# A hybrid decoder layer on one core: VectorE work cut and moved in the attention half, output weights prepared over three filler steps a block, and the gather placed ahead of the experts' choice

## The chip, the core and the metric

The kernel runs on one core of a Trainium2 chip. The metric is device time in microseconds for one execution of the whole layer. TensorE (PE) multiplies matrices into PSUM, VectorE (DVE), ScalarE (ACT) and GpSimd (POOL) work on tiles in SBUF and PSUM, and SyncE (SP) issues most of the transfers. Each engine runs its own list of instructions in order and waits for others by semaphores.

## The reference, cut to what matters

1024 tokens of width 1024 (S = D = 1024) go through one layer:

```
h    = rms_norm(x, norm1_w) * (1 + sc1) + sh1            # sh1, sc1, g1, sh2, sc2, g2 = silu(c) @ w_ada + b_ada
q, kv, gates, B, C, u = split(h @ w_in)                  # 512 + 6*128 + 24 + 3*512 columns
o    = sum over 3 branches of sigmoid(gate) * attention  # compressed blocks, 16 selected blocks, window of 512
                                                         # 8 query heads, 2 kv heads, bias by distance
y    = B * causal_conv3(C * u)
x    = x + g1 * (rms_norm per 64 columns of [o, y]) @ w_out
h2   = rms_norm(x, norm2_w) * (1 + sc2) + sh2
g    = argmax of 8 group probabilities; e1, e2 = best 2 of the group's 8 experts
x    = x + g2 * sum of g_prob * e_prob * (silu(h2 @ w1[e]) * (h2 @ w3[e])) @ w2[e]
```

There are 64 experts; their weights, w1 and w3 of 1024 x 512 and w2 of 512 x 1024 in float32, are 402.65 MB. All inputs and outputs are float32.

## The kernel before

**Order of the work.** The Python code issues instructions; a scheduler then orders them on each engine by what they wait for, so the code's order is only a start. `tc.issue_after(...)` pins an instruction behind another.

**Front (to about 228 us).** The adaLN vectors, the norm of x, and the first projections run. Projections are three float16 products each (high and low halves of both factors, L367 to L369). `cmp_post` makes the compressed keys: square on ScalarE, mean on VectorE, power -1/2 on GpSimd, scaling into `jk` on VectorE (L608), then a transpose on TensorE (L611). L193 is TensorE's work for the table of near biases and shares the PSUM tag `mx`. `rstd_of` (L635) gives 1/sqrt(mean square) for a 128 x 512 block with one Newton step, three VectorE instructions from L644 to L646.

**The attention loop (228 to 707 us).** A unit is one head on one half of the queries: units 0 to 7 are half 0, 8 to 15 half 1. Each unit has 9 (half 0) or 17 (half 1) slots, 208 in all. A slot is `scores` (TensorE into PSUM `st`), `weights` (two exponentials on ScalarE, P in float32 and PH in float16, then PL = P - PH, of six slots two on VectorE and four on GpSimd, L874) and, two slots later, `values` (PH and PL times the values into PSUM `acc`). At the end of each of a unit's three branches `take` divides by the sum and multiplies by the gate (L881 to L883, then L889 or L892). Between the slots run four other things:

- `prepare(u + 1)`: the row maxima of the next unit. QB gets a copy of the queries (L794); TensorE writes scores into `mx`; VectorE reduces them (L820, L835, L843) into `parts`; the compressed scores give the third maximum (L849) with a floor (L850); `Mh` (L852) goes back to TensorE (L857).
- `merge(pr)` after every second unit normalises two heads: square on ScalarE (L959), sum on VectorE, power on GpSimd (L964), multiply on VectorE (L965), and six slots later a transpose on TensorE (L971).
- In half 0 the filler `conv_steps`: projections and the short convolution, 2.75 steps a slot. Its post-processing is VectorE work (L746 to L763), the first tap at L748.
- In half 1 the filler `second_half`, 0.8 steps a slot. First `out_prepare`: eight blocks of 128 rows of w_out are scaled (L1075), rounded (L1077) and their rests taken (L1079, half on VectorE, half on GpSimd), one block a step. Then `out_part` (384 products L1121 to L1123 in all), `logits` and `route(0)` for the first 512 tokens, and `out_part` for the others. What the loop has not used up runs behind it.

**Transition (740 to 785 us).** `logits` of the last four token tiles, then `route(1)`: group choice G (L1186), the group's expert logits (L1191, L1194), top two (L1197, L1198), ranks by a triangular product (L1215, L1218), places, and one table product (L1271) with eight columns per row: token number, two expert places, two weights, a norm factor. Its result `tab0` gives the token numbers `toki0` (L1446); `rows_in(0)` gathers 2 x 128 rows by them (GpSimd, L1467); `group(0)` makes one-hot matrices Sm (L1484, L1485), the weights Sw (L1495 to L1497) and the scaled rows xh and xl (L1490, L1491); `take_in(0)` selects the rows of two experts by products (L1515) and applies the adaLN factors (L1520, L1523).

**Expert stage (to the end).** 32 pairs P of experts: `up(P)` (64 products, L1533), `silu_mul` (L1456), `down(P - 1)` (L1546), `turn(P)` (transposes of hid, L1556), `take_in(P + 1)`, `turn_weights`, `give`. The weights come in 2 MB transfers on SP in a fixed order through a handful of buffers (`stream`, `put`, L1024); a transfer into a buffer waits until the products that read it are done.

Of the kernel before, what the change touches and what calls it, by code (L numbers as in the profile page):

```python
# [69 lines left out]
def tile_layer(tc, A, out, dbg=None):  # L70
# [386 lines left out]
    V.tensor_scalar(nwc[:, 0:1], nwc[:, 0:1], HD ** -0.5 / WS, None, op0=ALU.mult)  # L457
    V.tensor_scalar(nwc[:, 1:3], nwc[:, 1:3], 1.0 / WS, None, op0=ALU.mult)
# [36 lines left out]
    tab0 = qa.tile([128, 2, 8], F32, name="tab0")  # L495
# [3 lines left out]
    V.memset(crow[:, :, 1:3], -1.0)  # L499

# [37 lines left out]
    def cmp_post(kvi):  # L538
        pw, w1n, w2n = (("cmp_pos_k", "cmp_k_w1", "cmp_k_w2"), ("cmp_pos_v", "cmp_v_w1", "cmp_v_w2"))[kvi]

        def post(p, b):
# [57 lines left out]
            if kvi == 0:  # L599
# [5 lines left out]
                ACT.activation(jk, pk[:, 0:64], AF.Square, accum_out=sk[:, 0:1])  # L605
                V.tensor_scalar(sk[:, 0:1], sk[:, 0:1], 1.0 / HD, EPS, op0=ALU.mult, op1=ALU.add)
                POOL.tensor_tensor(sk[:, 1:2], sk[:, 0:1], mhalf[:, 0:1], op=ALU.pow)
                V.scalar_tensor_tensor(jk, pk[:, 0:64], sk[:, 1:2], knc, op0=ALU.mult, op1=ALU.mult)  # L608
# [26 lines left out]
    def rstd_of(sq, tag="mx"):  # L635
# [9 lines left out]
        V.tensor_scalar(t, t, -0.5, 1.5, op0=ALU.mult, op1=ALU.add)  # L645
        V.tensor_mul(r, r, t)  # L646
# [49 lines left out]
    def gate_job(idx):  # L696
# [17 lines left out]
        V.reciprocal(gf, gf)  # L714
# [18 lines left out]
    def conv_steps():  # L733

        for i in range(4):
# [8 lines left out]
            def u_post(p, b, i=i, z=z, y=y):  # L744
# [3 lines left out]
                V.tensor_scalar(ys, zs, convw[:, i, 2:3], None, op0=ALU.mult)  # L748
# [5 lines left out]
            def b_post(p, b, i=i, y=y):  # L754
                ys = y[:, b * 512:(b + 1) * 512]
                V.tensor_mul(ys, p, ys)
                sq = square(ys, 1.0)
                yield
                yield
                r = rstd_of(sq)  # L760
                V.tensor_mul(ys, ys, r)
                ACT.activation(MH[b][:, 4 + i, :], ys, AF.Copy)
                V.tensor_sub(ML[b][:, 4 + i, :], ys, MH[b][:, 4 + i, :])  # L763
# [15 lines left out]
    for q in Tcs:  # L779
        V.memset(q, 0.0)  # L780
    ident2 = aw.tile([128, 128], F16, name="ident2", bufs=1)
    V.memset(ident2, 0.0)
    V.tensor_tensor(ident2[:, 0:63], identh[:, 0:63], identh[:, 64:127], op=ALU.add)
# [3 lines left out]
    def prepare(u):  # L787
# [6 lines left out]
        V.tensor_copy(QB[0:64, :], tq[hp:hp + 64, :])  # L794
# [54 lines left out]
        V.tensor_reduce(M[:, :, 2], pc[:, 0:256].rearrange("p (i n) -> p i n", i=4)[:, :, 0:63], axis=AX.X, op=ALU.max)  # L849
        V.tensor_scalar(M[:, :, 2], M[:, :, 2], MFLOOR, None, op0=ALU.max)  # L850
# [26 lines left out]
    def take(u, acc, n, gi):  # L877
# [3 lines left out]
        V.tensor_scalar(r, av[:, :, 64], 1e-27, None, op0=ALU.max)  # L881
        V.reciprocal(r, r)
        V.tensor_mul(r, r, gates[:, half * 4:half * 4 + 4, h * 3 + gi])  # L883
# [68 lines left out]
    def merge(pr):  # L952
# [12 lines left out]
        V.tensor_tensor(sq8, o8, so[:, :, None].to_broadcast([128, 8, 64]), op=ALU.mult)  # L965
# [88 lines left out]
    def out_prepare():  # L1054
# [16 lines left out]
        for i, k in enumerate(ORDER):  # L1071
# [8 lines left out]
            yield  # L1080
# [78 lines left out]
    def route(hb):  # L1159

        rt = R["rt"]
# [13 lines left out]
        def row(ap):  # L1175
            return ap[:, None, :].to_broadcast([128, 4, ap.shape[-1]])
        mx, ix = tile_(8, "mx"), tile_(8, "ix", U32)
# [4 lines left out]
        gid, gp, z, w0, w1c, pos, okg, t0, far = (W[:, :, i:i + 1] for i in (0, 3, 4, 5, 6, 9, 12, 15, 16))  # L1182
# [3 lines left out]
        V.tensor_tensor(G, row(io64[:, 0:8]), wide(gid, 8), op=ALU.is_equal)  # L1186
        ex = tile_(8, "ex")
# [6 lines left out]
        V.tensor_reduce(ein, el.rearrange("p t g e -> p t e g"), axis=AX.X, op=ALU.add)  # L1194
# [13 lines left out]
        V.tensor_copy(GA[:, ts, 0:8], G)  # L1208
        pr = ps(tag)

        if hb:
            PE.matmul(pr[:, 0:288], onesb, R["GS"][:, None, :].to_broadcast([128, 4, 72]), start=True, stop=True)
        for i in range(4):
            t = 4 * hb + i
            PE.matmul(pr[:, i * 72:(i + 1) * 72], trib, GA[:, t, :], start=(t == 0), stop=True,  # L1215
                      skip_group_check=True)
            if i < 3:
                PE.matmul(pr[:, (i + 1) * 72:288], onesb, GA[:, t:t + 1, :].to_broadcast([128, 3 - i, 72]),  # L1218
                          start=False, stop=True, skip_group_check=True)
# [498 lines left out]
```

## Time and profile before

| what | value |
|---|---|
| median of 3 runs | 1729.34 us (1725.88 to 1734.08) |
| the profiled execution | 1726.6 us |
| its span (first to last instruction) | 1724.8 us |
| granted TensorE clock in it, mean | 0.964 |
| busy: TensorE / VectorE / ScalarE / GpSimd | 1540.9 / 746.5 / 498.1 / 351.2 us |
| moved by DMA | 480.83 MB |

Rows of the timeline read: start, duration, engine, line, operation, output<-inputs, shape, and in brackets how long the engine had stood idle and what released it. Rows of groups read: count, then busy time and mean nanoseconds of one, then idle time ahead of them with its releasers. Rows of waits read: who waited for whom, total, times, longest.

### The profile page before, as it was taken

What the parts mean: (1) busy time and instruction counts of PE and PEld (TensorE: products, weight loads), DVE (VectorE), ACT (ScalarE), POOL (GpSimd) and SP (SyncE); (2) the same over time, 40 slices, a digit from 0 to 9 for tenths busy, and PEclk for the clock granted to TensorE, in tenths of its full rate; (3) what the DMA queues carried; (4) which work ended last, traced back from release to release, by engine and by line L of the source; (5) the groups of instructions that cost most, each with busy time, mean ns of one, the idle gap of its engine ahead of it and who ended that gap; (6) DMA issues with size and microseconds to landing.
All of it is one profiled execution on the core that took longest, in us unless ns stands there. A gap on an engine that the chain in (4) does not pass through costs nothing. (4 is left out here: it accounts for less than half of the span.)

```text
span 1724.8 us, 24591 instructions
## 1 busy us (share of the span) xinstructions
PE 1540.9 (89%) x9839; PEld 733.7 (43%) x9839; DVE 746.5 (43%) x1767; ACT 498.1 (29%) x968; POOL 351.2 (20%) x347
## 2 busy tenths in 40 slices
PE   5979899889879998959999999999999999899995
PEld 3434454445446665533434343343343333343431
DVE  3747876676796766554312223123203113121211
ACT  4654655445546564321112001011101002011000
POOL 4232543343454445220000000000000000000000
PEclk8989999999999999979999999999999999999998
DMA  9338531100241120759999999999999999999992
GB/s 348 100 113 258 179 92 34 51 23 15 69 151 41 35 79 22 299 196 395 421 426 425 428 426 426 428 425 427 427 426 426 428 425 427 425 427 427 426 428 122
DMA packets 84628, 480.83 MB, mean 279 GB/s; under 512 B 12551, under 2 KB 46552, under 8 KB 58652
## 3 DMA queue, kind: packets, MB, share of 16 engines
q1 hardware_dynamic: 76620, 461.16, 66.3%
q0 software_dynamic: 7744, 18.03, 2.9%
q8 instruction: 79, 1.29, 0.3%
q14 instruction: 41, 0.34, 0.1%
q10 hardware_dynamic: 144, 0.00, 0.0%
HBM read 473.20 MB, written 14.35 MB: 283 GB/s over the span
## 5 line engine op out<-in xcount | busy, mean ns | idle before, releaser
L1533 PE MATMUL ps<-wr,xs 128*64 128x512 f32 x2048 | 451.5, 596 | 0.0
L1546 PE MATMUL ps<-wr,hT 128*64 128x512 f32 x1024 | 260.3, 614 | 42.4 <-DMA wr<-in_w_dram 40.9
L1533 PEld LDWEIGHTS ps<-wr,xs 128*64 128x64 f32 x2048 | 158.3, 137 | 287.4 <-issue 251.7
L1520 ACT ACTIVATE xs<-ps,sh2p,a2p 128x128 f32<-128x128 f32 x128 | 55.0, 454 | 569.2 <-DVE xs L1523 569.1
L1456 DVE TENSOR_TENSOR hid<-ps,hid 128x512 f32<-128x512 f32 x32 | 22.1, 691 | 412.8 <-PE ps L1533 412.8
L1583 POOL DMA_INDIRECT out_dram<-xg,toki x16 | 15.9, 997 | 791.5 <-DVE xg L1582 790.8
L1546 PEld LDWEIGHTS ps<-wr,hT 128*64 128x64 f32 x1024 | 80.1, 141 | 215.4 <-issue 150.6
L874 POOL TENSOR_TENSOR PL<-P,PH 128x384 f16<-128x384 f32 (+3 forms) x138 | 128.5, 937 | 188.7 <-ACT PH L870 84.8
L1549 DVE TENSOR_TENSOR y<-ps,lt 128x512 f32<-128x512 f32 x64 | 44.3, 692 | 252.0 <-PE ps L1546 252.0
L868 ACT ACTIVATE P<-st 128x512 f32<-128x512 f32 (+3 forms) x208 | 98.4, 473 | 135.8 <-PE st L926 99.1
L1578 PE MATMUL sum<-y,CT 128*128 128x512 f32 x256 | 115.3, 593 | 0.0
L367 PE MATMUL pp<-hi,wh 128*128 128x512 f16 x272 | 106.0, 391 | 4.0 <-ACT hi L435 4.0
L368 PE MATMUL pp<-lo,wh 128*128 128x512 f16 x272 | 106.1, 390 | 0.0
L369 PE MATMUL pp<-hi,wl 128*128 128x512 f16 x272 | 105.8, 389 | 0.0
L870 ACT ACTIVATE PH<-st 128x512 f16<-128x512 f32 (+3 forms) x208 | 98.2, 472 | 3.1 <-DVE PL L874 2.0
L1455 ACT ACTIVATE hid<-ps 128x512 f32<-128x512 f32 x32 | 19.1, 597 | 200.9 <-PE ps L1533 200.9
L1515 PE MATMUL ps<-Sm,xh 128*128 128x128 f16 x512 | 62.4, 222 | 9.0 <-ACT xh L1490 9.0
L1578 PEld LDWEIGHTS sum<-y,CT 128*128 128x128 f32 x256 | 46.1, 190 | 46.8 <-issue 46.0
L1523 DVE TENSOR_SCALAR xs<-ps,a2p,sh2p 128x128 f32<-128x128 f32 x128 | 49.6, 407 | 35.5 <-ACT xs L1520 28.2
L1515 PE MATMUL ps<-Sm,xl 128*128 128x128 f16 x512 | 62.3, 222 | 1.8 <-DVE xl L1491 1.8
L945 PE MATMUL acc<-VH,PH 128*128 128x65 f16 x528 | 59.3, 196 | 4.2 <-DVE ot L892 4.0
L916 PE MATMUL st<-QA,KA 128*128 128x512 f16 (+1 forms) x192 | 61.5, 321 | 1.2 <-ACT PH L870 0.9
(438 smaller groups left out, 2546.5 us busy)
## 6 DMA issues: line engine op xcount, KB each, us to landing
wr<-in_w_dram SPq DMA_DIRECT2D x189, 2048.0 KB
ada<-in_w_ada_dram SPq DMA_DIRECT2D x32, 512.0 KB
raw<-in_w_in_dram SPq DMA_DIRECT2D x22, 512.0 KB
ada<-in_w_ada_dram SPq DMA_DIRECT2D x8, 1024.0 KB
xt<-in_x_dram SPq DMA_DIRECT2D x8, 512.0 KB
x<-in_w_out_dram SPq DMA_DIRECT2D x8, 512.0 KB
wr<-in_w_dram SPq DMA_DIRECT2D x3, 1024.0 KB
w1t<-in_cmp_k_w_dram POOLq DMA_DIRECT2D x4, 512.0 KB, 5.6
```

Source lines behind the costliest of these rows:

```text
L367: PE.matmul(p, wh[:, k, :], hi[:, k, m], start=(k == 0), stop=False)
L368: PE.matmul(p, wh[:, k, :], lo[:, k, m], start=False, stop=False)
L369: job_pe[0] = PE.matmul(p, wl[:, k, :], hi[:, k, m], start=False, stop=(k == KT - 1)).ins
L868: ACT.activation(P[:, c], p[:, c], AF.Exp)
L870: ACT.activation(PH[:, c], p[:, c], AF.Exp)
L874: eng.tensor_sub(PL[:, c], P[:, c], PH[:, c])
L916: PE.matmul(p[:, c], KA[g][:, j, b, :], tq[:, c], start=True, stop=False)
L945: PE.matmul(o, PH[:, w_], vh, start=(first and q == q0), stop=False, skip_group_check=True)
L1515: pe(PE.matmul(q[:, k * 128:(k + 1) * 128], part[:, a, h, k, :], Sm[:, a, sl], start=(a == 0 and part is xh), stop=(a == 1 and part is xl)))
L1533: pe(PE.matmul(hp_[nm][64 * u:64 * u + 64, :], xs[:, k, 64 * u:64 * u + 64], wring[nm, 2 * P + u, k], start=(k == 0), stop=(k == KT - 1)))
L1546: pe(PE.matmul(q[64 * u:64 * u + 64, :], hT[:, f, 64 * u:64 * u + 64], wring["w2", 2 * P + u, f][:, n * 512:(n + 1) * 512], start=(f == 0) ...
L1578: pe(PE.matmul(sums[a][n], CT[:, a, :], y[:, n * 512:(n + 1) * 512], start=(p == 0), stop=(p == 3)))
```

## The change

- `rstd_of`: two of the Newton step's VectorE instructions become one; the factor -0.5 goes into constants (`nwc`, MH, ML).
- Gates keep 1 + exp(-z) rather than its reciprocal, so `take` needs two small instructions instead of three.
- The floor of the compressed maximum goes into the product itself (a row of MFLOOR in Tc, 64 columns of ident2 instead of 63), and L850 goes.
- The QB copy and the first convolution tap move from VectorE to ScalarE.
- The merge's multiply moves from VectorE to GpSimd, behind the power.
- The compressed key is copied out of PSUM (`pks`) before its square.
- `out_prepare` yields three times a block.
- `route` is split: the group's ranks and a table of two columns (`tabA`: token number, norm factor) come first and give `toki0`; the experts' choice follows, with a table of four columns (`tab0`).
- `group(0)` first makes 128 columns of Sm; the other 384 and Sw (`held_back`) come behind the last `xs` of the second half. `up(0)` starts on the first half of the rows; the second half is taken in inside it. `turn_weights(0)` moves behind `turn(0)`.

```diff
@@ rstd_of
         V.scalar_tensor_tensor(t, m, EPS, t, op0=ALU.add, op1=ALU.mult)
-        V.tensor_scalar(t, t, -0.5, 1.5, op0=ALU.mult, op1=ALU.add)
-        V.tensor_mul(r, r, t)
+        V.scalar_tensor_tensor(r, t, 3.0, r, op0=ALU.subtract, op1=ALU.mult)
@@ cmp_post
-                ACT.activation(jk, pk[:, 0:64], AF.Square, accum_out=sk[:, 0:1])
+                pks = cp.tile([128, 64], F32, name="pks")
+                V.tensor_copy(pks, pk[:, 0:64])
+                ACT.activation(jk, pks, AF.Square, accum_out=sk[:, 0:1])
@@ gate_job
-        V.reciprocal(gf, gf)
@@ conv_steps
-                V.tensor_scalar(ys, zs, convw[:, i, 2:3], None, op0=ALU.mult)
+                ACT.activation(ys, zs, AF.Identity, scale=convw[:, i, 2:3])
@@ prepare
-        V.tensor_copy(QB[0:64, :], tq[hp:hp + 64, :])
+        ACT.activation(QB[0:64, :], tq[hp:hp + 64, :], AF.Copy)
...
-        V.tensor_scalar(M[:, :, 2], M[:, :, 2], MFLOOR, None, op0=ALU.max)
@@ take
-        V.tensor_scalar(r, av[:, :, 64], 1e-27, None, op0=ALU.max)
+        V.scalar_tensor_tensor(r, av[:, :, 64], 1e-27, gates[:, half * 4:half * 4 + 4, h * 3 + gi],
+                               op0=ALU.max, op1=ALU.mult)
         V.reciprocal(r, r)
-        V.tensor_mul(r, r, gates[:, half * 4:half * 4 + 4, h * 3 + gi])
@@ merge
         POOL.tensor_tensor(so, so, mhalf, op=ALU.pow)
-        V.tensor_tensor(sq8, o8, so[:, :, None].to_broadcast([128, 8, 64]), op=ALU.mult)
+        POOL.tensor_tensor(sq8, o8, so[:, :, None].to_broadcast([128, 8, 64]), op=ALU.mult)
@@ out_prepare
-            yield
+            for _ in range(3):
+                yield
@@ route
         V.tensor_tensor(G, row(io64[:, 0:8]), wide(gid, 8), op=ALU.is_equal)
+        V.tensor_copy(GA[:, ts, 0:8], G)
+        pg = ranks(ps(tag), 0, 8)
...
+        table(tabA, payA3, 2, tabA if hb else crow[:, :, 6:8].to_broadcast([128, 2, 2]))
+        if hb:
+            V.tensor_copy(toki0, tabA[:, :, 0])
+        yield
...
+        pe_ = ranks(ps(tag), 8, 64)
...
+        table(tab0, payB3, 4, tab0 if hb else crow[:, :, 1:5].to_broadcast([128, 2, 4]))
@@ group
+        places(slice(0, 512 if g else 128))
...
+        if g:
+            weights_of()
+        else:
+            held_back.append(weights_of)
@@ up
+                if P == 0 and nm == "w1" and k == 3:
+                    take_in(0, (1,))
+                    with tc.issue_after(last_xs[0]):
+                        held_back.pop()()
@@ before the loop over pairs
-    take_in(0)
-    turn_weights(0)
+    take_in(0, (0,))
@@ in the loop
             turn(P)
+        if P == 0:
+            turn_weights(0)
```

`ranks` holds the same products as L1213 to L1219 before, for some of the columns; `table` those of L1271 with the sum behind it; `places` and `weights_of` the lines L1484 to L1497.

VectorE at a merge of half 0 (the second of the eight), before and then after. `so` and `osq` belong to the merge, `MHL` and `y` to the convolution, `M`, `Mh` and `parts` to the next unit's maxima, `rr` to `take`:

```order
L763 TENSOR_TENSOR MHL<-y,MHL 128x512 [waits Activation_49]
L965 TENSOR_TENSOR osq<-oN,so 128x512 [waits Pool_49]
L849 TENSOR_REDUCE M<-mx 128x4 [waits PE_49]
L851 TENSOR_REDUCE M<-parts 128x4x2 [waits DVE_49]
L850 TENSOR_SCALAR M<-M 128x4 [waits DVE_49]
L807 MEMSET parts 128x32 [waits DVE_49]
L852 TENSOR_SCALAR Mh<-M 128x4x3 [waits DVE_49]
L881 TENSOR_SCALAR rr<-acc 128x4 [waits PE_49]
```

```order
L766 SCALAR_TENSOR_TENSOR MHL<-y,MHL 128x512 [waits Activation_49]
L853 TENSOR_REDUCE M<-mx 128x4 [waits PE_49]
L854 TENSOR_REDUCE M<-parts 128x4x2 [waits DVE_49]
L855 TENSOR_SCALAR Mh<-M 128x4x3 [waits DVE_49]
L811 MEMSET parts 128x32
L884 SCALAR_TENSOR_TENSOR rr<-acc,gates 128x4 [waits PE_49]
```

The multiply and its wait for GpSimd no longer stand ahead of the maxima. On GpSimd it now stands between the power and the next PL:

```order
L967 TENSOR_TENSOR so<-so,mhalf 128x8 [waits DVE_49]
L968 TENSOR_TENSOR osq<-oN,so 128x512 [waits Activation_49,Pool_49]
L877 TENSOR_TENSOR PL<-P,PH 128x512 [waits PE_49,Activation_49]
L344 TENSOR_TENSOR wl<-raw,wh 128x1024 [waits PE_49,Activation_49]
L877 TENSOR_TENSOR PL<-P,PH 128x384 [waits Activation_49]
```

Before, the power was followed directly by that PL.

VectorE where the output weights are prepared (fourth to sixth block before, sixth and seventh after; `x` is a block of w_out, `WHL` its halves):

```order
L1075 SCALAR_TENSOR_TENSOR x_5146<-x_5146,vcols,g1bc 128x1024 [waits DMAHW3_49,Pool_49]
L883 TENSOR_TENSOR rr<-rr,gates 128x4 [waits DVE_49]
L849 TENSOR_REDUCE M<-mx 128x4 [waits PE_49]
L1075 SCALAR_TENSOR_TENSOR x_5207<-x_5207,vcols,g1bc 128x1024 [waits DMAHW4_49,Pool_49]
L1079 TENSOR_TENSOR WHL_5030<-x_5146,WHL_5030 128x512 [waits Activation_49]
L1075 SCALAR_TENSOR_TENSOR x_5241<-x_5241,vcols,g1bc 128x1024 [waits DMAHW5_49,Pool_49]
L1079 TENSOR_TENSOR WHL_5029<-x_5207,WHL_5029 128x512 [waits Activation_49]
```

```order
L1078 SCALAR_TENSOR_TENSOR x_5436<-x_5436,vcols,g1bc 128x1024 [waits DMAHW7_49]
L824 ISA jq,parts<-mx,nearQ 128x256 [waits PE_49]
L824 ISA parts 128x1
L839 TENSOR_REDUCE parts<-mx 128x2 [waits PE_49]
L824 ISA jq,parts<-mx,nearQ 128x256 [waits DVE_49]
L824 ISA parts 128x1
L1082 TENSOR_TENSOR WHL_4983<-x_5436,WHL_4983 128x512 [waits Activation_49]
L877 TENSOR_TENSOR PL<-P,PH 128x128 [waits Activation_49,Pool_49]
L839 TENSOR_REDUCE parts<-mx 128x2 [waits PE_49]
L847 TENSOR_REDUCE parts<-mx 128x1 [waits PE_49]
L1078 SCALAR_TENSOR_TENSOR x_5561<-x_5561,vcols,g1bc 128x1024 [waits DMAHW2_49]
```

Maxima and PL now stand between the blocks; from the first block's scaling to the last's there are 31 rows before and 68 after.

VectorE at the transition: before, the token numbers are cast from the full table, behind the last two one-hots `oh`; after, from `tabA` (`t_9451` is its sum), among the first instructions of the experts' choice (`ein`, `me`, `ie`):

```order
L1264 TENSOR_SCALAR pay_9496<-W_9451 128x4x2
L1302 TENSOR_TENSOR W_9451<-W_9451 128x4x2
L1262 TENSOR_TENSOR pay_9501<-W_9451,pay_9501 128x4x2 [waits DVE_49]
L1303 TENSOR_SCALAR W_9451<-W_9451 128x4x2 [waits DVE_49]
L1304 TENSOR_TENSOR W_9451<-W_9451 128x4x2 [waits DVE_49]
L1269 TENSOR_SCALAR oh_9534<-io,W_9451 128x256 [waits PE_49]
L1269 TENSOR_SCALAR oh_9538<-io,W_9451 128x256 [waits PE_49]
L1278 TENSOR_REDUCE t_9542<-st 128x16 [waits PE_49]
L1279 TENSOR_TENSOR tab_542<-tab_542,t_9542 128x16 [waits DVE_49]
L1446 CAST toki_9559<-tab_542 128x2 [waits DMAHW1_49,DVE_49]
```

```order
L1238 TENSOR_SCALAR oh_9438<-io,W_9407 128x256
L1238 TENSOR_SCALAR oh_9440<-io,W_9407 128x256
L1252 TENSOR_REDUCE ein<-el 128x32
L1212 TENSOR_REDUCE t_9451<-st 128x4 [waits PE_49]
L1255 MAX me<-ein 128x8 [waits DVE_49]
L1255 MAX me<-ein 128x8
L1213 TENSOR_TENSOR tabA<-t_9451,tabA 128x4 [waits DVE_49]
L1256 MAX_INDEX ie<-me,ein 128x8 [waits DVE_49] x2
L1242 CAST toki_543<-tabA 128x2 [waits DVE_49]
L1255 MAX me<-ein 128x8 x2
```

The cast of the token numbers moved ahead of the experts' choice, and no longer waits for a transfer.

## Prediction before the changed kernel was run

> **What bounds the kernel now.** I read the page first: shares, the slices, the expert stage's costliest group and the transfers behind it.
>
> ```profile
> PE 1540.9 (89%) x9839; PEld 733.7 (43%) x9839; DVE 746.5 (43%) x1767; ACT 498.1 (29%) x968; POOL 351.2 (20%) x347
> ...
> PE   5979899889879998959999999999999999899995
> ...
> GB/s 348 100 113 258 179 92 34 51 23 15 69 151 41 35 79 22 299 196 395 421 426 425 428 426 426 428 425 427 427 426 426 428 425 427 425 427 427 426 428 122
> ...
> L1546 PE MATMUL ps<-wr,hT 128*64 128x512 f32 x1024 | 260.3, 614 | 42.4 <-DMA wr<-in_w_dram 40.9
> ```
>
> A slice is 1724.8 / 40 = 43.1 us. From slice 19 (counting from 1) to the last but one the transfers hold 395 to 428 GB/s, and 40.9 of the 42.4 us for which TensorE stands idle ahead of the down projection go to the expert weights: that stage, 900 us and more, ends when its last weight lands. The change leaves those bytes alone, so it can pay only through the moment at which the weight stream starts again after slice 18 (196 GB/s), and that moment is the end of everything before. There the windows say how full TensorE is:
>
> ```profile
> core 0: us, PE busy (x) PEld busy (x) DVE busy (x) ACT busy (x) POOL busy (x), PEclk, DMA share, GB/s
> 230.00:340.00 110.00, 100.17 (x778) 54.41 (x777) 71.24 (x194) 54.89 (x112) 44.80 (x42) 0.97 0.15 41
> 340.00:450.00 110.00, 102.02 (x808) 55.76 (x806) 77.47 (x213) 52.82 (x110) 43.08 (x39) 1.00 0.08 21
> 450.00:510.00 60.00, 42.54 (x342) 23.21 (x342) 52.63 (x103) 31.63 (x61) 32.75 (x30) 0.89 0.50 157
> 510.00:600.00 90.00, 82.10 (x954) 55.34 (x953) 64.75 (x204) 53.87 (x126) 46.19 (x50) 0.98 0.11 36
> 600.00:700.00 100.00, 90.17 (x1034) 59.81 (x1033) 64.50 (x236) 56.34 (x134) 47.76 (x54) 0.98 0.16 53
> ```
>
> TensorE's idle time in the attention loop is 9.83 + 7.98 + 17.46 + 7.90 + 9.83 = 53.0 us: the most that relief on other engines can give there. The third window is the bad one: TensorE 71% busy, VectorE 52.63 / 60 = 88%. What the two engines wait for there (the loop from 228 us on for VectorE; 230 to 450, then 450 to 700 us for TensorE; total, times, longest):
>
> ```profile
> DVE QB L794 <- PE st L910: 20.8, 10, 4.8
> DVE osq L965 <- POOL so L964: 13.2, 7, 3.0
> ```
>
> ```profile
> PE mx L857 <- DVE Mh L852: 6.7, 3, 2.9
> ```
>
> ```profile
> PE mx L832 <- DVE parts L820: 11.6, 6, 3.4
> PE acc L948 <- POOL PL L874: 3.3, 3, 2.2
> PE pp L1123 <- DVE WHL L1079: 2.6, 3, 1.1
> PE mx L971 <- DVE W L1259: 2.1, 1, 2.1
> ```
>
> VectorE, which runs its instructions in order, stands 34.0 us still at two lines (the copy of the queries, the multiply of the merge), and TensorE waits mostly for maxima that are queued on VectorE. One merge as VectorE ran it, and one later row:
>
> ```profile
> 301.15 1.40 DVE L965 TENSOR_TENSOR osq<-oN,so 128x512 f32<-128x512 f32 x1 [3.03 <-POOL so L964]
> 302.48 2.60 DVE L763 TENSOR_TENSOR MHL<-y,MHL 128x512 f16<-128x512 f32 x1
> ...
> 305.19 0.18 DVE L852 TENSOR_SCALAR Mh<-M 128x12 f16<-128x12 f32 x1
> ...
> 361.90 1.64 DVE L850 TENSOR_SCALAR M<-M 128x4 f32<-128x4 f32 x1
> ```
>
> 3.03 us of waiting for the power on GpSimd and 1.40 of multiply, all ahead of the row maximum Mh that TensorE wants: the three waits for Mh (6.7 us) stand behind three such merges. The last row is one of the removed floors: 128x4 elements, here 1.64 us.
>
> **The change part by part, in order of time.** *A, front (to 228 us).* Norms lose one VectorE pass (20 of them), the reciprocal of the gates goes, and the compressed key leaves PSUM before its square.
>
> ```profile
> PE mx L193 <- DVE jk L608: 8.2, 1, 8.2
> ...
> PE mx L857 <- DVE Mh L852: 3.0, 1, 3.0
> ```
>
> ```profile
> 213.78 1.48 DVE L850 TENSOR_SCALAR M<-M 128x4 f32<-128x4 f32 x1
> ...
> 215.22 0.38 DVE L645 TENSOR_SCALAR t<-t 128x512 f32<-128x512 f32 x1
> 109.28 0.58 PE L193 MATMUL mx<-nf,exch 128*128 128x512 f16 x1 [8.16 <-DVE jk L608]
> 109.67 0.63 PE L367 MATMUL st<-hi,wh 128*128 128x512 f16 x1
> ```
>
> The 8.2 us are a wait for the PSUM buffer that jk reads. With the early copy the second L193 no longer waits, but three rows of projection later the transpose wants jk itself, and what delays jk (ScalarE, behind a load) is untouched. What moves ahead of the stall is one L193 and three projection matmuls: 0.58 + 3 x 0.38 = 1.7 us by their durations (0.38 is a matmul of this size at full clock, quoted below at 707 us); bounds 0 (jk later by the copy) and 8.2 (ScalarE comes early). The floor and the norm pass ahead of Mh are 1.48 + 0.38 of the 3.0 us waited there; I take 1.3. **A = -3** (0 to -9).
>
> *B, half 0 of the loop (228 to 451 us), 17.8 us idle.* Of the three waits for Mh (6.7) I take 5 as gone, and a third of the other 11 us, since VectorE drops some 4 short instructions a unit and half of its 20.8 us at L794. Against it stand ScalarE, which takes over copies and the first convolution tap, and GpSimd, which takes the multiply; their prices by the nearest rows:
>
> ```profile
> L643 ACT ACTIVATE t<-r 128x512 f32<-128x512 f32 x9 | 5.6, 626 | 0.1
> ...
> L965 DVE TENSOR_TENSOR osq<-oN,so 128x512 f32<-128x512 f32 x8 | 9.6, 1196 | 15.0 <-POOL so L964 15.0
> ...
> L1079 POOL TENSOR_TENSOR WHL<-x,WHL 128x512 f16<-128x512 f32 x8 | 11.1, 1392 | 10.6 <-ACT WHL L1077 10.4
> L1079 DVE TENSOR_TENSOR WHL<-x,WHL 128x512 f16<-128x512 f32 x8 | 8.1, 1014 | 0.7 <-ACT WHL L1077 0.7
> ```
>
> ScalarE: 8 taps x 0.63 = 5.0 us and 16 half-height copies, on an engine that is 50% busy in these windows (54.89 of 110): a third of the taps, some 2 us, I count as felt. GpSimd: the multiply, 1.20 us on VectorE, by the row of equal shape 1.39, between 1.2 and 1.7; it stands in front of the PL subtractions, for which TensorE waits 3.3 us in half 1 already. I count 1 us felt in each half. GpSimd is 41% busy (44.80 of 110), which is the cover; gone, it costs 4 x 1.4 = 5.6 us a half. **B = -5 - 4 + 2 + 1 = -6** (+3 to -12).
>
> The Trainium skill, "GPSIMD Engine Reference", § 3.1, speaks against this step: it gives an elementwise addition of two fp32 operands as 1.96 times slower on GpSimd than on VectorE and keeps "use DVE for elementwise" as the rule. By that ratio the multiply would be an estimated 1.96 x 1.20 = 2.3 us and the eight of them 7.7 us dearer than by the row; if all of that were felt, the sum would be 1710. Here the two engines' rows of one shape stand at 1392 against 1014 ns, 1.37 times.
>
> *C, half 1 and the rest up to the logits (451 to 740 us).* (1) The weights of the output projection: the third window idles 17.46 us, where the rate of the two windows behind it (17.7 of 190) would give 5.6. The eight blocks now stand in 68 of VectorE's instructions rather than 31, about twice as far apart, not three times as the loop over the filler says. I take 9 of the 11.9 us. (2) Three merges at other places: the waits at L832 (11.6 us, 6 times) in part: -4. (3) Routing of the first half, a burst of tiny VectorE instructions (the 2.1 us at L971 is one of several waits), falls later, where no maxima are prepared: -3.5. (4) The rest of the relief: -3. (5) Price: the filler loses 16 steps to empty yields, so by the order 69 of the 384 output matmuls go from inside the loop to behind it (123 behind before, 192 now).
>
> ```profile
> 707.35 0.38 PE L1121 MATMUL pp<-WHL,MHL 128*128 128x512 f16 x1
> ...
> 718.35 0.38 PE L1121 MATMUL pp<-WHL,MHL 128*128 128x512 f16 x1
> ```
>
> 51 matmuls start between these rows, 11.00 / 51 = 0.216 us each: 69 cost 14.9 us behind the loop. Inside, I let 70% of that go back, because TensorE is over 90% busy there and the fill was mostly on its path: -10.4. Both ends, 0 and 100%, stay for the range. The last merge now has fewer matmuls to hide power and multiply: +2, between 0 and 4. **C = -9 - 4 - 3.5 - 3 - 10.4 + 14.9 + 2 = -13** (+7 to -26).
>
> *D, transition to the experts (740 to 785 us).* In order of time, DVE, TensorE, GpSimd, ScalarE:
>
> ```profile
> 740.40 0.19 DVE L1186 TENSOR_TENSOR G<-io,W 128x32 f32<-128x32 f32 x1
> 744.05 0.22 PE L1215 MATMUL st<-GA,trib 128*128 128x72 bf16 x1 [4.70 <-DVE GA L1206]
> 749.85 0.17 DVE L1446 CAST toki<-tab 128x2 int32<-128x2 f32 x1
> 750.84 1.54 POOL L1467 DMA_INDIRECT xg<-x1D,toki  x1 [11.59 <-DVE Sw L1495]
> 756.01 2.31 ACT L1490 ACTIVATE xh<-xg,tab 128x512 f16<-128x512 f32 x2 [12.88 <-DMA xg<-x1D,toki]
> 764.59 14.76 PE L1533 MATMUL ps<-wr,xs 128*64 128x512 f32 x64
> 781.75 0.75 PE L1556 MATMUL ps<-identf,hid 128*128 128x128 f32 x4 [2.40 <-DVE hid L1456]
> ```
>
> From the group one-hot G to the token numbers, 62 VectorE instructions take 9.45 us, 0.15 each with their waits. The order leaves about 21 there, 3.2 us, and two trips to TensorE that nothing covers now, some 0.8 each: 4.8 us, so the numbers come 4.7 earlier, at 745.2, and with them gather (746.1) and xh (751.3). The experts' table comes later than before, since some 15 instructions of the group's part now stand ahead of it (15 x 0.15 = 2.3 us): 752 instead of 749.7, about with the gathered rows. From xh to the first up projection there were 8.6 us (756.01 to 764.59); with the second half of the rows put behind the first projections, about half of one 2.31 us row of ScalarE goes from this stretch: 751.3 + 7.4 = 758.7, 5.9 us earlier. The held-back columns and Sw (near 5 us on VectorE) then run under the 14.76 us of up(0), and hid stands behind them: if they are late, the transposes of hid are, not the stream, whose buffers come free by up(0). **D = -5.5** (-7 to 0).
>
> Sum: -3 - 6 - 13 - 5.5 = -27.5 us. The profiled execution took 1726.6 us (span 1724.8 and 1.8 around it): 1699.1. The median of the runs shown, 1729.34, lies 2.7 above it: about **1702 us**, likeliest case alone 1692 to 1712.
>
> **Rivals.** *R1, the loop keeps its pace* (other side). If a slot is set by the round trip scores, exponential, PL, values and not by fill, taking matmuls out gives nothing, and a multiply in front of PL lengthens it. Place: GpSimd's queue at the merges. For it: L948 waits for GpSimd's PL, up to 2.2 us. Against: TensorE over 90% busy in four of the five windows. Price: A -3, B and C's relief nothing, +14.9 + 2 behind the loop, 7 x 1.4 = +9.8 at the merges, D -5.5: +18, so 1747. The point from which it decides: the change loses when the loop from 228 us on shrinks by less than 16.9 - 3 - 5.5 = 8.4 us, merges included; a loop that neither shrinks nor grows gives 1738.
>
> *R2, the merge stays a stall*: GpSimd's pow and multiply in one row (1.7 + 1.4 us) delay PL as much as VectorE delayed Mh, so the 5 + 4 us of merges come back: 1711. If VectorE's relief fails with it in the third window too, 1720. *R3, D is hidden*: gather or hid late, 1707. *R4, relief in full*: the loop's 53 us of idle time fall to 16 in place of the 32 that the sum leaves (53.0 - 6 in B, - 19.5 + 4.5 in C): 1686. *R5, the spread is undone*: the scheduler pulls the weight blocks forward as it already does by half; C1 falls to 0: 1711.
>
> **How the numbers follow.** Forecast 0.50; R2 and R5 together 0.20 (0.04 of it above 1720.7); R3 0.10; R4 0.08; R1 0.12, half of it within 0.5%. 0.5% is 8.6 us, about what a measurement of this kernel tells from no change: 1720.7 to 1738.0. Faster 0.50 + 0.16 + 0.10 + 0.08 = 0.84, same 0.04 + 0.06 = 0.10, slower 0.06. The range 1686 to 1722 leaves out R1 and the tails.
>
> **What the changed profile would show.** Right: TensorE idle in the loop near 32 us; VectorE without a wait for the power; the weight blocks' stretch above 80% busy on TensorE; the last scores some 39 us earlier (A, B and the terms of C inside the loop), the logits some 22; the first up projection 18 us after G rather than 24; expert stage as long as before, weights at 425 GB/s. Wrong: waits for PL on GpSimd above 10 us (R2), a loop of 478 us still, 228 to 706 (R1), the stream starting later than hid's gain says (R3).

## The result, and the profile after

The changed kernel takes 1702.02 us in the median of four runs (1699.76 to 1705.03), the kernel before 1729.05 (1725.88 to 1734.08, four runs by now). The ratio is 0.9842, 95% interval 0.9825 to 0.9859: 27 us, 1.6%, faster. The profiled execution took 1703.64 us (span 1701.9).

The page of the changed kernel: busy time, TensorE and GB/s in 40 slices, and the costliest group of the down projection (L1546 before):

```profile
PE 1537.3 (90%) x9870; PEld 733.9 (43%) x9870; DVE 711.5 (42%) x1678; ACT 512.3 (30%) x992; POOL 356.8 (21%) x355
...
PE   5978988999889998969999998999999999899995
...
GB/s 352 102 114 261 155 110 44 36 39 17 64 158 46 40 33 188 246 257 399 427 425 427 427 424 428 426 426 427 427 427 427 427 426 426 426 426 429 426 428 112
...
L1590 PE MATMUL ps<-wr,hT 128*64 128x512 f32 x1024 | 258.0, 608 | 44.3 <-DMA wr<-in_w_dram 42.8
```

VectorE has 35.0 us less work (746.5 to 711.5), ScalarE 14.2 and GpSimd 5.6 more. The expert stage is the one of before: 424 to 429 GB/s, and 42.8 of 44.3 us of idle time there are for weights. So the gain was made ahead of it. Windows cut at the ends of the stages show where (columns as in the prediction; before, then after: half 0 of the loop, half 1, from the last `take` to the group choice G, from G to the first up projection):

```profile
230.00:457.00 227.00, 207.29 (x1625) 112.62 (x1623) 153.76 (x416) 113.72 (x232) 90.84 (x83) 0.98 0.13 36
457.00:700.00 243.00, 209.71 (x2287) 135.91 (x2287) 176.83 (x533) 135.83 (x308) 123.73 (x132) 0.96 0.22 68
700.00:740.00 40.00, 37.08 (x223) 22.68 (x222) 21.12 (x53) 7.77 (x14) 7.52 (x9) 1.00 0.93 370
740.00:765.00 25.00, 6.37 (x51) 4.91 (x52) 19.92 (x84) 5.77 (x8) 9.34 (x8) 0.55 0.43 157
```

```profile
226.00:455.00 229.00, 211.75 (x1642) 115.57 (x1641) 136.36 (x372) 125.28 (x252) 91.08 (x85) 0.97 0.14 40
455.00:666.00 211.00, 190.61 (x2247) 128.44 (x2246) 162.32 (x489) 138.00 (x313) 128.97 (x136) 0.98 0.25 80
666.00:723.00 57.00, 51.03 (x281) 28.61 (x277) 25.79 (x63) 8.00 (x15) 9.29 (x11) 0.97 0.68 258
723.00:739.00 16.00, 4.63 (x47) 3.28 (x46) 14.51 (x75) 4.74 (x5) 8.48 (x9) 0.56 0.57 206
```

Half 0 is no shorter, half 1 is 32 us shorter, the stretch behind the loop is 17 us longer (69 output matmuls moved behind the last scores, 59 of them behind the last `take`), and the transition is 8 to 9 us shorter. By the exact times of the timeline the two profiled executions differ by: first exponential -3.4 (229.6 to 226.2), half 0 +0.7, half 1 -31.7, tail +17.0, transition -8.2, first up projection to the end +2.6; together -22.9, the difference of the spans. The medians differ by 27; single executions lie up to 5 us from theirs.

Half 1's 31.7 us are not waits alone. TensorE's listed idle time falls by 13.8 us (33.6 to 19.8, table below; 1.7 of the 33.6 lie just ahead of half 1); the 59 matmuls, at the 0.216 us each of the prediction, make 12.7; and the granted clock is 0.98 instead of 0.96, which by the rows above is an estimated 243 x 0.04 - 211 x 0.02 = 5.5 us. What lowers the clock is left open here.

Waits of the changed kernel, VectorE from 228 to 700 us, then TensorE from 228 to 668 us:

```profile
DVE rr L884 <- PE acc L951: 24.2, 10, 4.1
...
DVE t L649 <- ACT t L648: 12.4, 6, 4.2
...
DVE y L753 <- ACT y L751: 5.0, 4, 2.3
```

```profile
PE acc L951 <- DVE PL L877: 5.6, 7, 1.6
PE acc L951 <- POOL PL L877: 5.5, 8, 1.4
PE acc L948 <- DVE ot L895: 5.2, 3, 3.0
PE acc L306 <- DVE acc L295: 4.4, 1, 4.4
```

VectorE now waits mostly for TensorE's results, which is as it should be, and no longer for the power. The wait for ScalarE's tap (L751) is new, and the one for its square (L648) has grown from 5.5 us. On TensorE the 11.6 us for parts at L832 are gone from the head of the list. In their place stand waits for PL, from both engines that make it. The last row is a single wait at 234.18 us, just behind the first exponential: TensorE wants the last adaLN vector, which VectorE has only now finished. The kernel before has no such wait.

### The profile page after: what moved, and what is told of

The parts are those of the page before. It is cut to its first block, busy times and chain, and to the rows that moved or that the text cites. A ratio compares the mean times of both kernels' runs of the same rounds, so it can differ in the third digit from the quotient of the medians.

```text
span 1701.9 us, 24631 instructions
## 1 busy us (share of the span) xinstructions
PE 1537.3 (90%) x9870; PEld 733.9 (43%) x9870; DVE 711.5 (42%) x1678; ACT 512.3 (30%) x992; POOL 356.8 (21%) x355
## 5 line engine op out<-in xcount | busy, mean ns | idle before, releaser
L1590 PE MATMUL ps<-wr,hT 128*64 128x512 f32 x1024 | 258.0, 608 | 44.3 <-DMA wr<-in_w_dram 42.8
L1593 DVE TENSOR_TENSOR y<-ps,lt 128x512 f32<-128x512 f32 x64 | 44.3, 692 | 250.3 <-PE ps L1590 250.3
L1484 ACT ACTIVATE hid<-ps 128x512 f32<-128x512 f32 x32 | 19.1, 597 | 197.2 <-PE ps L1573 197.2
```

Source lines behind the costliest of these rows:

```text
L1590: pe(PE.matmul(q[64 * u:64 * u + 64, :], hT[:, f, 64 * u:64 * u + 64], wring["w2", 2 * P + u, f][:, n * 512:(n + 1) * 512], start=(f == 0) ...
```

## The experiments

Each kernel's ratio is to the kernel before on the same chip, with its 95% interval; the changed kernel's is 0.9842 (0.9825 to 0.9859). "Idle" is TensorE's idle time ahead of matmuls, summed from the timeline of a profile (gaps above 0.15 us): before 18.4 us in half 0 (first exponential to unit 7's last `take`) and 33.6 in half 1, after 17.1 and 19.8.

| kernel | median us | ratio | interval | idle half 0 | idle half 1 | tail, last take to G | G to up(0) |
|---|---|---|---|---|---|---|---|
| before | 1729.05 | 1 | | 18.4 | 33.6 | 39.9 | 24.2 |
| after | 1702.02 | 0.9842 | 0.9825-0.9859 | 17.1 | 19.8 | 56.9 | 16.0 |
| only_f | 1716.41 | 0.9932 | 0.9915-0.9949 | 13.7 | 27.2 | 40.2 | 23.5 |
| no_f | 1712.62 | 0.9909 | 0.9892-0.9927 | 19.2 | 26.8 | 56.6 | 16.0 |
| no_abc | 1712.77 | 0.9913 | 0.9894-0.9932 | 17.4 | 27.5 | 55.4 | 16.4 |
| no_c | 1701.69 | 0.9849 | 0.9828-0.9870 | 16.0 | 20.5 | 55.4 | 17.5 |
| only_h | 1729.26 | 1.0002 | 0.9987-1.0016 | 19.7 | 31.7 | 53.6 | 24.9 |
| no_h | 1706.17 | 0.9869 | 0.9844-0.9895 | 16.5 | 21.2 | 40.9 | 16.0 |
| only_T | 1730.57 | 1.0001 | 0.9986-1.0016 | 19.1 | 37.1 | 40.5 | 16.0 |
| no_T | 1706.79 | 0.9862 | 0.9834-0.9890 | 16.2 | 19.9 | 55.6 | 23.9 |
| no_de | 1697.81 | 0.9825 | 0.9807-0.9842 | 12.5 | 21.2 | 55.3 | 16.6 |
| no_e | 1699.36 | 0.9830 | 0.9807-0.9852 | 14.3 | 18.3 | 55.3 | 17.7 |
| best1 | 1701.65 | 0.9846 | 0.9825-0.9868 | 10.5 | 20.1 | 55.4 | 16.1 |
| best1_fill | 1695.34 | 0.9810 | 0.9788-0.9832 | 10.7 | 20.0 | 40.6 | 16.0 |

The first exponential is an uncertain border for half 0: where the loop begins earlier, part of the front's waiting falls behind it, at L306. The same profiles, cut at the last `take` of unit 0 and that of unit 7, in us:

| kernel | wait at L306 behind the first exponential | unit 0's last take at | units 1 to 7 | idle in them |
|---|---|---|---|---|
| before | 0 | 260.6 | 196.9 | 17.0 |
| after | 4.4 | 265.4 | 189.4 | 11.1 |
| only_f | 0 | 264.6 | 188.6 | 12.1 |
| no_f | 4.1 | 264.2 | 191.4 | 14.3 |
| no_abc | 0 | 262.2 | 193.4 | 15.2 |
| no_c | 4.2 | 264.2 | 187.8 | 10.8 |
| no_de | 1.0 | 262.8 | 186.6 | 10.6 |
| no_e | 3.4 | 264.1 | 187.2 | 10.4 |
| best1 | 0 | 262.9 | 187.4 | 9.8 |

### only_f and no_f: the merge's multiply

only_f is the kernel before with this one line, no_f the changed kernel without it:

```diff
-        V.tensor_tensor(sq8, o8, so[:, :, None].to_broadcast([128, 8, 64]), op=ALU.mult)
+        POOL.tensor_tensor(sq8, o8, so[:, :, None].to_broadcast([128, 8, 64]), op=ALU.mult)
```

> The kernel before with the merge's multiply on GpSimd, nothing else. Theory, the multiply and its wait stand in front of the maxima: the waits for Mh and parts behind merges go, TensorE's idle time in the loop falls by 6 to 8 of 52 us, time 1722. Rival, GpSimd delays PL by as much: idle in the loop within 2 us of before, waits for GpSimd's PL up by 5, time 1729.

> The changed kernel with the merge's multiply back on VectorE. Theory: idle time in the loop 6 to 8 us above the changed kernel's 34.7, time 1709. Rival, with the rest of VectorE relieved the multiply costs nothing there (and PL comes earlier): within 2 us of the changed kernel, 1702.

Alone the line is worth 12 us (ratio 0.9932), and taking it out of the changed kernel costs 11. TensorE's waits in only_f from 228 to 700 us, and the row of the same window in the kernel before that is not shown yet:

```profile
PE acc L948 <- POOL PL L874: 8.9, 7, 3.6
...
PE mx L832 <- DVE parts L820: 2.8, 3, 1.7
```

```profile
PE mx L857 <- DVE Mh L852: 8.4, 5, 2.9
```

The waits for parts at L832 fall from 11.6 to 2.8 us and those for Mh at L857 from 8.4 to under 2.5, too little to be listed; those for GpSimd's PL rise from 3.3 to 8.9. The rival's wait exists, then, but gives back a third. GpSimd's multiply, all eight in the changed kernel (duration min/median/max in ns, first and last start):

```profile
L968 POOL TENSOR_TENSOR osq<-oN,so x8: 1031/1042/1047, 301.0 to 672.0; 128x512 f32<-128x512 f32 x8
```

### no_abc and no_c: the short instructions

no_abc puts back the Newton step's second pass, the reciprocal of the gates, the third instruction of `take`, and the floor; no_c the floor alone. The undone lines, the floor last:

```diff
-        V.scalar_tensor_tensor(r, t, 3.0, r, op0=ALU.subtract, op1=ALU.mult)
+        V.tensor_scalar(t, t, -0.5, 1.5, op0=ALU.mult, op1=ALU.add)
+        V.tensor_mul(r, r, t)
...
+        V.reciprocal(gf, gf)
...
-        V.scalar_tensor_tensor(r, av[:, :, 64], 1e-27, gates[:, half * 4:half * 4 + 4, h * 3 + gi],
-                               op0=ALU.max, op1=ALU.mult)
+        V.tensor_scalar(r, av[:, :, 64], 1e-27, None, op0=ALU.max)
         V.reciprocal(r, r)
+        V.tensor_mul(r, r, gates[:, half * 4:half * 4 + 4, h * 3 + gi])
...
+        V.tensor_scalar(M[:, :, 2], M[:, :, 2], MFLOOR, None, op0=ALU.max)
```

> The changed kernel with the short VectorE instructions put back: the second pass of the Newton step, the reciprocal of the gates, the third instruction of each take, the floor of the maxima. Theory, their number matters, each one can be held until a running GpSimd instruction ends: 6 us slower, 1708, the larger part in half 0, where the norms lie. Rival, 85 instructions of 0.15 to 0.5 us beside other work cost nothing: within 2 us.

> The changed kernel with the floor of the compressed maximum as its own VectorE instruction again, 16 times 128x4. Theory, it stands right ahead of Mh and can be held until a running GpSimd instruction ends, so that it costs 0.15 to 1.6 us each time: 3 to 5 us slower, 1706, near half of what the short instructions together gave (10.7). Rival, a single short instruction is lost in the noise: within 2 us.

Together they are worth 11 to 12 us, as much as the multiply. The floor, whose 1.64 us row the prediction shows, is worth nothing by itself. And the larger part of the gain lies in half 1 (idle 27.5 instead of 19.8, time 220.5 instead of 211.4 us); units 1 to 7 take 193.4 us instead of 189.4, though the norms lie in half 0 and the front. In half 1 only the takes and the floors were put back, so `take` is left as the likely place: it stands between TensorE's last product into `acc` and the reuse of that buffer. Its instruction that was put back, in no_abc, beside the one that took its place in the changed kernel (duration min/median/max in ns):

```profile
L888 DVE TENSOR_TENSOR rr<-rr,gates x48: 153/429/2084, 247.9 to 676.5; 128x4 f32<-128x4 f32 x48
```

```profile
L884 DVE SCALAR_TENSOR_TENSOR rr<-acc,gates x48: 124/156/164, 250.2 to 666.2; 128x4 f32<-128x4 f32 x48
```

The 48 take 25.0 us on VectorE in no_abc. Of them 26 last over 0.2 us, and each of these ends within 0.04 us of a GpSimd instruction that was running when it started; the last section has such a pair. In the changed kernel none lasts over 0.164 us. The floor was held in the same way, but without it the hold falls on the instruction that makes Mh: in no_abc the floor took up to 1.81 us and Mh at most 0.40, in the changed kernel Mh took up to 1.32 (in no_c both up to 1.1). That fits a floor worth nothing. `take` was not tried alone.

### only_h and no_h: the output weights spread over three steps

```diff
-            yield
+            for _ in range(3):
+                yield
```

> The kernel before with three filler steps for each block of output weights, nothing else. Theory, the stretch of units 8 and 9 was bound by VectorE's weight preparation: units 8 and 9 take 60 us instead of 75, TensorE idle there falls by 9 us, time 9 us lower (1720), although 69 matmuls go behind the loop. Rival, VectorE stays overloaded by the short instructions and the merges: units 8 and 9 take 70 or more, time within 3 us of before.

> The changed kernel with one filler step a block, as before. Theory: units 8 and 9 take some 68 us again, 9 us above the changed kernel (1711). Rival, the relief of VectorE alone clears the stretch: within 3 us of the changed kernel.

Alone: nothing (1.0002). The windows of only_h, half 1 and tail:

```profile
458.00:687.00 229.00, 197.78 (x2242) 130.45 (x2243) 179.23 (x531) 135.25 (x308) 126.35 (x133) 0.97 0.23 73
687.00:740.00 53.00, 48.85 (x268) 27.95 (x266) 23.84 (x57) 7.76 (x14) 4.60 (x7) 0.97 0.73 278
```

Half 1 is 14 us shorter than before (243 to 229) and the tail 13 us longer (40 to 53): the matmuls moved, 53 of the 69 across the last `take`, at about the same price at either place, and little else happened (idle in half 1 31.7 us instead of 33.6). Units 8 and 9 take 71.2 us instead of 74.2, not 60. In the changed kernel the spread is worth 4 us by the medians (1706.17 to 1702.02), but the intervals overlap; there units 8 and 9 take 64.8 us with it and 69.2 without.

### only_T and no_T: the transition

only_T is the kernel before with the split `route`, the early gather, the 128 columns first and the first up projection in two parts; no_T the changed kernel without them. Of the edit the decisive lines:

```diff
+        table(tabA, payA3, 2, tabA if hb else crow[:, :, 6:8].to_broadcast([128, 2, 2]))
+        if hb:
+            V.tensor_copy(toki0, tabA[:, :, 0])
...
-    take_in(0)
-    turn_weights(0)
+    take_in(0, (0,))
```

> The kernel before with the transition part alone (split route, early gather, partial Sm, up(0) in two halves). Theory, the gain is real and adds up: G to the first up projection 16 us instead of 24, the weight stream starts 6 to 7 us earlier, time 6 us below before (1723). Rival, hidden (the stream's restart hangs on something else): within 1.5 us of before.

> The changed kernel with the transition as it was before. Theory: 6 us above the changed kernel, 1708, about 21 below before; last exponential at the same 659 us as in the changed kernel. Rival, the transition's gain came from the attention half (the routing of the first half, which is split too): 1712 and the last exponential later by some us.

The transition of the changed kernel, in order of time as in the prediction:

```profile
723.08 0.19 DVE L1223 TENSOR_TENSOR G<-io,W 128x32 f32<-128x32 f32 x1
726.47 0.15 DVE L1242 CAST toki<-tabA 128x2 int32<-128x2 f32 x1
727.44 1.15 POOL L1496 DMA_INDIRECT xg<-x1D,toki  x1 [4.42 <-DVE OI L1329]
732.06 4.53 ACT L1521 ACTIVATE xh<-xg,tabA 128x512 f16<-128x512 f32 x4 [4.65 <-PE st L1209]
739.09 5.01 PE L1573 MATMUL ps<-wr,xs 128*64 128x512 f32 x16 [0.51 <-DVE xs L1563]
757.65 0.63 PE L1600 MATMUL ps<-identf,hid 128*128 128x128 f32 x3 [1.52 <-DVE hid L1485]
```

G to the token numbers takes 3.4 us instead of 9.45, G to the first up projection 16.0 instead of 24.2. only_T has the same 16.0:

```profile
747.56 0.19 DVE L1222 TENSOR_TENSOR G<-io,W 128x32 f32<-128x32 f32 x1
...
763.55 1.12 PE L1572 MATMUL ps<-wr,xs 128*64 128x512 f32 x2 [0.51 <-DVE xs L1562]
```

Yet it is no faster than before (1.0001): its G stands at 747.56 instead of 740.40. Half 1 takes 247.3 us instead of 243.1, with 3.5 us more idle time, most of it in units 14 and 15 (61.1 us instead of 56.9), where the routing of the first half, which is split too, works among the maxima; another 1.9 us come from the front, which nothing changed. In the changed kernel, with VectorE relieved, half 1 is as long without the split (211.8) as with it (211.4), and the transition's gain arrives: 1706.79 without, 1702.02 with it, with intervals that overlap. That the loop takes the gain back only while VectorE is crowded fits these profiles; it was not tried by itself.

### no_de and no_e: the two copies moved to ScalarE

no_de puts the QB copy and the first tap back on VectorE, no_e the tap alone:

```diff
-                ACT.activation(ys, zs, AF.Identity, scale=convw[:, i, 2:3])
+                V.tensor_scalar(ys, zs, convw[:, i, 2:3], None, op0=ALU.mult)
...
-        ACT.activation(QB[0:64, :], tq[hp:hp + 64, :], AF.Copy)
+        V.tensor_copy(QB[0:64, :], tq[hp:hp + 64, :])
```

> The changed kernel with the QB copy and the first convolution tap back on VectorE. Theory, VectorE standing at the copy (20.8 us before) is what held the maxima: 5 us slower, 1707, idle in both halves up. Rival, that standing was slack (VectorE had nothing to do that TensorE wanted): within 2 us; ScalarE with fewer instructions might even win 1 or 2.

> The changed kernel with the first convolution tap alone back on VectorE; the QB copy stays on ScalarE. Theory, the tap is the loss: VectorE, in order, waits for ScalarE's tap (5.0 us) and for the square of the norms behind it (12.4 instead of 5.5 us before); without the tap half 0 idles 10 us as with both back, time 1698. Rival, the QB copy is the loss (it stands among the exponentials): time 1702, half 0 idling 15.

Neither is slower, and no_de, at 1697.34 to 1699.42, lies below every run of the changed kernel. VectorE's waits in no_de:

```profile
DVE QB L798 <- PE st L913: 16.4, 8, 3.5
...
DVE t L649 <- ACT t L648: 5.7, 4, 3.3
```

VectorE stands 16.4 us at the copy again, and half 0 idles less (12.5 us instead of 17.1): it stood there with nothing that TensorE wanted. What the move made worse for VectorE are the waits for ScalarE's square (12.4 us, now 5.7) and its tap (5.0, now none). For TensorE little of that counts: of the 4.6 us, 3.4 are the wait at L306 at the loop's start (4.4, now 1.0), and in units 1 to 7 the idle time is 10.6 us instead of 11.1. The size in time stays open: best1, below, has the same lines back and measured 1701.65.

### best1 and best1_fill: the memset in pieces, and more filler

Both start from no_de; best1_fill has the second edit as well:

```diff
-    POOL.memset(xgs[0], 0.0)
+    for a_ in range(2):
+        for c_ in range(4):
+            POOL.memset(xgs[0][:, a_, c_ * 256:(c_ + 1) * 256], 0.0)
...
-FILL = (2.75, 0.8)
+FILL = (2.75, 0.95)
```

> The changed kernel with QB copy and tap back on VectorE and the 128x2048 memset of the gathered rows (GpSimd, 1.80 us, during which a 128x4 cast of VectorE took 1.71) in eight pieces of 128x256. Theory, VectorE's cast is held until the GpSimd instruction running at its start ends: the cast takes under 0.5 us, G comes 1.3 us earlier after the last logits (1.2 instead of 2.5 us), time 1 to 1.5 us below the kernel without the pieces (1696.5). Rival, the cast is slow by itself: 1.7 us again, no gain.

> The same as best1 with 0.95 filler steps a slot in half 1 instead of 0.8, so that 65 of the 192 output matmuls behind the loop go back into it. Theory, the loop is bound by TensorE's work, so that they cost inside what they cost behind: last exponential some 14 us later, tail 14 us shorter, time within 3 us of best1, 2 us lower at best through filled gaps. Rival, the loop keeps its pace whatever it is given (its round trip sets it): the last exponential stays, time 10 us lower. Other rival, the fill crowds the maxima: slower by over 3 us.

best1 decides nothing on the memset. In its profile the pieces begin at 719.16, after the cast has ended, and in no_de, with the memset whole, it began after the cast too; so there was no hold to take away, and the predicted gain did not come. The rows of best1 (GpSimd, VectorE):

```profile
719.16 2.38 POOL L1473 MEMSET xg<- 128x256 f32 x8 [7.87 <-DMA x1D<-xp]
...
718.56 0.17 DVE L1221 CAST W<-ix 128x4 f32<-128x4 uint32 x1
```

best1_fill has the lowest median of all, 1695.34 us, below both; its interval overlaps with theirs. Half 1 and tail, best1 and then best1_fill:

```profile
450.00:663.00 213.00, 192.60 (x2238) 128.40 (x2236) 164.08 (x496) 133.90 (x304) 128.24 (x135) 0.98 0.25 79
663.00:719.00 56.00, 51.26 (x288) 28.82 (x285) 24.54 (x65) 8.00 (x15) 7.73 (x10) 0.97 0.69 263
```

```profile
451.00:675.00 224.00, 203.18 (x2312) 134.73 (x2310) 161.18 (x502) 133.83 (x304) 132.37 (x136) 0.99 0.24 75
675.00:715.00 40.00, 36.69 (x210) 22.24 (x209) 20.25 (x55) 7.78 (x14) 8.43 (x16) 0.96 0.90 368
```

By the exact times of the last `take` and of G the tail shrank by 14.7 us and half 1 grew by 10.4: inside the loop the matmuls cost 70% of their price behind it. The rest did not fill the listed waits: TensorE's idle time in half 1 is as long with them (20.0 us) as without (20.1). Some of it is the granted clock, 0.99 instead of 0.98 in half 1, by these rows an estimated 213 x 0.02 - 224 x 0.01 = 2 us; the remainder is open. The rival of a loop that keeps its pace whatever it holds is out.

## Why the prediction was right, point by point

The time came out at the forecast, 1702; several terms of the sum did not. By the two profiled executions A and B together brought 2.7 us instead of 9, C 14.7 instead of 13 (with two misses that cancelled) and D 5.6 instead of 5.5: 22.9 for 27.5. That the medians lie 27 apart, and meet the forecast to a tenth, is luck within the scatter of single executions.

- **A, front, -3: not there.** The first exponential came 3.4 us earlier, but unit 0's last `take` 4.8 us later. Behind the first exponential TensorE stands 4.4 us at L306 for the last adaLN vector, which VectorE finishes at 234.1 us, before at 231.8. The failed step is the one that counts shorter waits in the front as time won: what half 0 needs next was not ready any earlier. Four profiles with the front of before have that `take` at 260.6 to 264.6 us, five with the whole new front (after, no_f, no_h, no_T, no_e) at 261.9 to 266.5. The key's stall did what the prediction said: it moved behind three projection matmuls and lost little. TensorE's waits in the front of the changed kernel:

```profile
PE mx L616 <- DVE jk L613: 5.1, 1, 5.1
...
PE mx L193 <- DVE pks L609: 1.9, 1, 1.9
```

5.1 + 1.9 = 7.0 us instead of 8.2.

- **B, half 0, -6.** From the first exponential half 0 lasted 0.7 us longer, but this stretch holds the wait at L306. Units 1 to 7 took 7.5 us less (196.9 to 189.4) and idled 5.9 less, so the size was about right. The merges are in it (only_f: 8.3 us less than before; the changed kernel without its multiply, no_f: 2.0 more) and the short instructions (no_abc: 4.0 more). Wrong was the step that took half of VectorE's 20.8 us at L794 for lost time: with the copy and the tap back on VectorE, units 1 to 7 take 186.6 us, no more than with them on ScalarE. A wait of an engine that nobody waits for is no reserve.
- **C, half 1 and tail, -13.** Measured -31.7 + 17.0 = -14.7, close, by other terms. C1, 9 us for the spread, failed: alone it is worth nothing, since half 1 gives back just the price of the moved matmuls. The row with VectorE at 88% busy was read as the weight blocks' fault. Units 8 and 9, where these blocks stand, before and after:

```profile
457.50:531.80 74.30, 57.11 (x560) 34.49 (x561) 66.05 (x154) 41.27 (x88) 42.32 (x43) 0.91 0.41 128
```

```profile
454.80:519.60 64.80, 52.22 (x558) 32.95 (x556) 61.60 (x141) 43.08 (x90) 48.65 (x45) 0.95 0.41 131
```

  VectorE is busy for 89% before and for 95% after: the stretch is 9.5 us shorter, and VectorE is still the fuller engine in it. With the short instructions back these two units take 70.4 us (no_abc), with the merge's multiply back 65.7 (no_f). Merges and short instructions, 4 + 3 us for half 1 in the sum, were sized too small: putting the multiply back lengthens half 1 by 8.0 us (no_f, 219.4), putting the short instructions back by 9.1 (no_abc, 220.5). The sum also has no term for the granted clock and calls 53.0 us of idle time the most that relief can give, though its third window shows a clock of 0.89; half 1 won an estimated 5.5 us there. C5, 70% of 14.9 us back, is what best1_fill shows (10.4 of 14.7); in only_h it was all of it. The tail, +16.9, came to +17.0, in part by chance: 59 matmuls instead of 69 crossed the last `take` (12.7 us), and the granted clock behind it was 0.97 instead of 1.00.
- **D, transition, -5.5.** -8.2 to the first up projection, and +2.6 from there to the end, together -5.6. The token numbers came 6.1 us earlier against G, not 4.7: the sum had 21 instructions and two uncovered trips to TensorE at 4.8 us, and they took 3.4. Not foreseen was that the split of the routing costs the loop some 4 us when it is made alone (only_T).
- **Rivals.** R1 is out: the loop shrank, by 31 us. R2's wait for GpSimd's PL exists, 5.5 us in the changed kernel and 8.9 in only_f, against 3.3 before, and stays small; the multiply takes 1.04 us, not the 1.39 estimated from L1079. The Trainium skill, "GPSIMD Engine Reference", § 3.1, has GpSimd 1.96 times slower than VectorE for an fp32 addition of 2048 elements. Here, at 512, GpSimd's 1.04 us stand against 0.69 to 1.65 us of the same multiply on VectorE, 1.5 times the shortest and less than the 1.20 mean. R4 did not come: the loop idles 17.1 + 19.8 = 36.9 us, where the sum leaves 32. R3 and R5 are half right: D alone and C1 alone gave nothing, but D did give its part in the changed kernel, by the medians.

## What to carry to other kernels

Of an in-order engine's waits only those count behind which something is queued that the bounding engine wants: the 13 us at the merge's power, with the 9.6 us of the multiply itself, were worth 12 us, the 21 us at the copy nothing. What a part is worth on a crowded engine depends on what else has gone from it: the spread and the transition were each worth nothing alone, and some 4 us in the changed kernel, by medians whose intervals overlap. Taken out of the changed kernel one at a time (no_f, no_abc, no_h, no_T, no_de), the parts come to 10.6 + 10.8 + 4.2 + 4.8 - 4.2 = 26 us by the medians, near the 27 of the whole. Moving filler out of a loop that TensorE bounds only moves time; moved back in, it cost 10.4 us for 14.7 here. And an earlier start counts only at the next point where everything is needed: the first exponential came earlier, the end of unit 0 did not.

## What the runs showed of the hardware that was not expected

A VectorE instruction of 0.17 us can last as long as a GpSimd instruction that runs when it starts. The cast ahead of G (128x4) took 0.17 us in eleven of the fourteen profiles; in the other three the memset on GpSimd had begun 0.11, 0.04 and 0.02 us before it. The rows, GpSimd and VectorE, of the changed kernel, of no_f and of no_T:

```profile
721.22 1.80 POOL L1471 MEMSET xg<- 128x2048 f32 x1 [7.15 <-DMA x1D<-xp]
721.33 1.71 DVE L1221 CAST W<-ix 128x4 f32<-128x4 uint32 x1
```

```profile
729.74 1.80 POOL L1471 MEMSET xg<- 128x2048 f32 x1 [7.23 <-DMA x1D<-xp]
729.78 1.79 DVE L1221 CAST W<-ix 128x4 f32<-128x4 uint32 x1
```

```profile
719.80 1.80 POOL L1444 MEMSET xg<- 128x2048 f32 x1 [7.26 <-DMA x1D<-xp]
719.82 1.81 DVE L1185 CAST W<-ix 128x4 f32<-128x4 uint32 x1
```

721.33 + 1.71 = 723.04 and 721.22 + 1.80 = 723.02; 731.57 and 731.54 in no_f, 721.63 and 721.60 in no_T: all three casts end with the memset. The floor of 1.64 us that the prediction shows, 361.90 to 363.54, ends with a GpSimd row of the kernel before as well, at 363.51:

```profile
360.95 2.56 POOL L344 TENSOR_TENSOR wl<-raw,wh 128x1024 f16<-128x1024 f32 x1
```

And so does the third instruction of `take` where it is put back; the first of no_abc, 249.88 beside 249.85:

```profile
247.72 2.13 POOL L344 TENSOR_TENSOR wl<-raw,wh 128x1024 f16<-128x1024 f32 x1 [1.06 <-ACT wh L342]
247.90 1.98 DVE L888 TENSOR_TENSOR rr<-rr,gates 128x4 f32<-128x4 f32 x1
```

Not every instruction is held: VectorE searched for maxima at 738.22 in 0.16 us while the memset of the kernel before ran (737.44 to 739.24).

```profile
737.44 1.80 POOL L1443 MEMSET xg<- 128x2048 f32 x1 [4.53 <-DMA x1D<-xp]
738.22 0.16 DVE L1180 FIND_INDEX8 ix<-mx,L 128x8 uint32<-128x8 f32 x1
```

The Trainium skill, "SBUF — State Buffer", § Who interferes with whom, says this of casts and scalar operations: they can take the port pair that VectorE shares with GpSimd, and whoever comes second waits for the whole instruction of the first. The rows of the cast and of the floor agree. So the changed kernel pays some 1.5 us on its critical path in executions where the memset begins just ahead of the cast; a kernel that keeps them apart for certain was not run.
